# Branch-operand splits tied behind a weight and taken later; the low parts of all weights formed on VectorE

## The chip, the cores and the metric

The kernel runs on one core of one Trainium2 chip. The metric is the device time of one execution in microseconds (us). The engines are TensorE (PE, matrix products), VectorE (DVE), ScalarE (ACT), GpSimd (POOL) and SyncE (SP, whose queue starts most of the loads and stores). Each runs its own list of instructions in order and waits for the others through semaphores. What the scheduler decides is the order within each list.

## What is computed

One layer of a hybrid encoder over two sequences of 256 tokens, 1024 channels, in fp32, cut to what matters here:

```
h = rmsnorm(x);  proj = h @ w_in      -> qkv, ab, z_gdn, cq, ckv, z_mla, q_mem, z_mem, gate_logits
A: q,k,v = silu(conv5(qkv));  o_f, o_b = gated_delta_rule (chunks of 64, forward and backward), 8 heads
   o_gdn = rmsnorm(o_f + o_b) * silu(z_gdn)
B: latent attention, 8 heads, rotary keys, full softmax            o_mla = ... * silu(z_mla)
C: cross-attention into 256 memory tokens, 4 heads                 o_mem = ... * silu(z_mem)
merged = sig(g0)*(o_gdn @ w_br_gdn) + sig(g1)*(o_mla @ w_br_mla) + sig(g2)*(o_mem @ w_br_mem)
y = rmsnorm(x + merged @ w_out)
```

## The kernel before

All 512 tokens lie on the free axis and channels on the 128 partitions, so a product of one weight tile has 128 output channels by 512 tokens. Each fp32 operand is held as a rounded high part and a low part (operand minus high part). A product is three passes: high activations times high weight (`hh`, `wh`), low activations times high weight (`hl`, `wh`), high activations times low weight (`hh`, `wl`), 24 matmuls of 128x512 for 1024 input channels.

`weight` (L195) brings one weight tile in. SP loads it into the raw tile `wr_name` (two buffers), ACT rounds it to `wh_name` (two buffers, L206, remembered as `self.wround`), and one engine subtracts to form `wl_name` (two buffers, L213). That engine is POOL, in steps of 256 columns, for names that begin with q (`qkv`, `qm`, `qn`) and for `km3`; for the others it is DVE, in one instruction, which is remembered as `self.wsplit`. The next load into a raw buffer waits until both its rounding and its subtraction are done. `split` does the same for an activation: ACT writes the high part (L221), DVE the low part (L223, or L225 with a scale).

The program has three stages. `front` (to about 383 us) runs the memory attention, the latent attention (softmax tiles `p_m`, `ph_m`, `p_a`) and products between them; there the scheduler sets the order on all engines. `middle` (to about 745 us) is the gated delta rule. Its function `weave` merges chains of steps (lanes that solve heads, their loads, norms, the preparation of four heads at a time in `gdn_prep`) with a list of fill products. Each chain yields a planned time, the fill list fills the time between, and PE's order is written by hand from this. `back` has the last projections and the output. A convolution on a product tile is a copy `cz` (ACT L735), five shifted multiply-adds on DVE (`kq`, `vf`, L744 and L746) and copies on ACT.

A lane's solve goes back and forth between the engines: PE `u` (L1080), ACT `u` and `ub` (L1082, L1085), PE `xs` (L1090), DVE `w` (L1094), PE `us` (L1099), ACT `ub` (L1102), PE `o` and `x`, DVE `vs` (L1075). `gdn_prep` inverts triangular blocks on DVE with 31 pairs `tm`, `tt` (L870, L872), then transposes and copies into `t32` and `y32` (L893 to L901).

`xe` is the gated output of the memory branch and `xa` that of the latent attention. Both were written to HBM as `d_xm` and `d_xa`. `load_xe` and `load_xa` bring tiles back, `split_x` and `split_xa` halve and split them, and `branch_mem` (weights `be`) and `branch(1, ...)` (weights `bm`) multiply them with a branch weight. All are entries of the fill list; `can` says which may be taken at the planned time `now`: a `split_xa` of parts 0 to 4 when 6 planned us have passed since its load, a `split_x` at once when its turn comes. Instructions under `issue_after(i)` are placed behind instruction `i` in the order of their engine.

Of the kernel before, what the change touches and what calls it, by code (L numbers as in the profile page):

```python
# [7 lines left out]
F32 = mybir.dt.float32  # L8
F32R = mybir.dt.float32r
AF = mybir.ActivationFunctionType  # L10
ALU = mybir.AluOpType
# [4 lines left out]
D = 1024  # L16
KD = D // P
EPS = 1e-6
NEG = -1e30


# [19 lines left out]
def _consts():  # L41
# [8 lines left out]
    for tb in range(2):  # L50
# [8 lines left out]
        ("trf", m <= i32), ("trb", m >= i32), ("i32", m == i32),  # L59
        ("ngf", np.where(i32 > m, 0.0, NEG)), ("ngb", np.where(i32 < m, 0.0, NEG)),  # L60
        ("one", np.ones((P, 1))), ("hf", np.full((P, 4), -0.5)), ("ph", np.full((P, 16), 0.5)),
# [93 lines left out]
class Layer:  # L155
# [34 lines left out]
    def c(self, n):  # L190
        lo, hi = _OFF[n]
        return self.cst[:, lo:hi]


    def weight(self, src, n, name, pool=None):  # L195

        nc = self.nc
        raw = self.p0.tile([P, 1024], F32, tag="wr", bufs=2, name="wr_" + name)
        with self.tc.high_priority(offset=1000):
            d = nc.sync.dma_start(raw[:, :n], src)  # L200
        if name == "bg2":
            self.after = d.ins
        kw = {} if pool else {"tag": "wh", "bufs": 2}
        hi = (pool or self.p0).tile([P, 1024], F32R, name="wh_" + name, **kw)
        with self.tc.high_priority(offset=60):
            self.wround = nc.scalar.activation(hi[:, :n], raw[:, :n], AF.Copy).ins  # L206
            kw = {} if pool else {"tag": "wl", "bufs": 2}
            lo = (pool or self.p0).tile([P, 1024], F32R, name="wl_" + name, **kw)
            eng = nc.gpsimd if name[0] == "q" or name == "km3" else nc.vector
            step = 256 if eng is nc.gpsimd else n  # L210
            for q in range(0, n, step):
                t = slice(q, min(n, q + step))
                d = eng.tensor_tensor(lo[:, t], raw[:, t], hi[:, t].bitcast(F32), op=ALU.subtract)  # L213
            if eng is nc.vector:
                self.wsplit = d.ins
        return hi, lo
# [44 lines left out]
    def mean_cols(self, acc, n, name):  # L261
# [5 lines left out]
        r = self.p0.tile([P, 4], F32, tag="c4", bufs=4, name="ms_" + name)  # L267
        nc.vector.tensor_scalar(r, ss[:, 0:4], 1.0 / n, EPS, ALU.mult, ALU.add)
        return r
# [506 lines left out]
    def gdn_prep(self, g):  # L776
# [4 lines left out]
        nc, c = self.nc, self.c  # L781
# [33 lines left out]
        with self.tc.high_priority(offset=0 if g else 900):  # L815
            for h in range(4):
                for s in range(2):
                    for cc in range(2):
                        w = h * 4 + s * 2 + cc
                        for a in range(4):  # L820
                            t = slice(cc * P + 32 * a, cc * P + 32 * a + 32)
# [11 lines left out]
        nc.vector.tensor_reduce(k2, tmp, axis=AX.X, op=ALU.add)  # L833
        nc.vector.tensor_scalar(k2, k2, 4 * EPS, None, ALU.add)
        nc.vector.reciprocal(rc, k2)
# [14 lines left out]
        for d in range(2):  # L850
            t = self.tb(f"nd{g}{d}").rearrange("p (w i) -> p w i", i=32)
# [15 lines left out]
        for i in range(31):  # L867
            n, m = 31 - i, i + 1
# [5 lines left out]
        ts = self.pb.tile([P, 32, 32], F32, tag="blk", bufs=3, name=f"ts{g}")  # L874
# [14 lines left out]
        for a in range(4):  # L889
            r = slice(32 * a, 32 * a + 32)  # L890
            d = a % 2
            with self.tc.issue_after(self.wround):
                nc.scalar.activation(t32[r], (o2 if d else o1)[r, :, 16 * d:16 * d + 16].rearrange("p i u -> p u i"),  # L893
                                     AF.Copy)
            yield 0.0, 6.0 if g else 2.8
        with self.tc.issue_after(self.wround):
            nc.scalar.activation(y32[:, 0:16], o2[:, :, 0:16].rearrange("p i u -> p u i"), AF.Copy)
        yield 0.0, 6.0 if g else 2.8
        for q in range(2):
            with self.tc.issue_after(self.wround):  # L900
                nc.scalar.activation(y32[:, 16 + q:32:2], o1[:, :, 17 - q:32:2].rearrange("p i u -> p u i"), AF.Copy)  # L901
            yield 0.0, 6.0 if g else 2.8
        self.ready[g] = self.now + 4
        return t32, y32, cc

# [18 lines left out]
    def decay_mask(self, es):  # L924
        for d, e in enumerate(es):
# [3 lines left out]
            for r in (slice(o, o + 128), slice(256, 384)):  # L929
                self.nc.gpsimd.affine_select(out=e[:, :, r], in_=e[:, :, r], pattern=[[0, 2], [sg, 128]],  # L930
                                             compare_op=ALU.is_ge, fill=NEG, base=0, channel_multiplier=-sg)

# [173 lines left out]
    def gdn_out(self, hh):  # L1106
# [33 lines left out]
        rr = self.rr[:, 0:4]  # L1140
        nc.vector.tensor_scalar(rr, ssp[:, 0:4], 1.0 / 128, 128 * EPS * EPS, ALU.mult, ALU.add)  # L1141
        nc.gpsimd.tensor_tensor(rr, rr, c("hf")[:, 0:4], op=ALU.pow)  # L1142
# [92 lines left out]
    def output(self):  # L1235
# [26 lines left out]
        def add(ps, tb, half, n=512):  # L1262
            y = ys[tb][:, half * n:(half + 1) * n]
            nc.vector.tensor_tensor(y, y, ps, op=ALU.add)
            i = half if n == 512 else half - 1
            nc.scalar.activation(self.ct("jk")[:, :n], y, AF.Square, accum_out=ss[tb][:, i:i + 1])
            return y
# [7 lines left out]
        for tb in range(4):  # L1275
            y = add(pss[tb], tb, 0)
            nc.vector.tensor_scalar(ss[tb][:, 0:1], ss[tb][:, 0:1], 1.0 / D, EPS, ALU.mult, ALU.add)
            nc.gpsimd.tensor_tensor(y, y, fg[:, 0:512], op=ALU.mult)
# [225 lines left out]
    def can(self, f, *a):  # L1504

        if f == self.load_xa:
            return (3 in self.ub and self.pr[1], 5 in self.ub and 7 in self.hd, 6 in self.ub and 7 in self.hd,
                    7 in self.started, self.out > 6 and 7 in self.started, 7 in self.ub)[a[0]]
        if f == self.split_xa:
            return self.now > self.xa_at.get(a[0], 1e9)  # L1510
        if f == self.branch_mem and a[0] == 7:
            return 5 in self.xa_raw
        return f != self.branch or None not in self.xa
# [42 lines left out]
    def load_xe(self, f):  # L1556

        t = self.big(f, f"xe{f}")
        self.nc.sync.dma_start(t[:, 1].bitcast(F32), self.d_xm[:, f])
        self.xe.append((t[:, 0], t[:, 1]))  # L1560
        yield 0.0

    def split_x(self, xs):
        for hi, lo in xs:
            self.split(lo.bitcast(F32), hi, lo, 0.5)
        yield 0.0

    def load_xa(self, part):

        lo, tags = ((0, ("y32",)), (1, ("na",)), (2, ("na", "y0")), (4, ("y32",)), (5, ("ub",)), (6, ("na", "y1")))[part]  # L1570
        ts = [self.pg.tile([P, 2, 512], F32R, tag=t, bufs={"na": 3, "y0": 1, "y1": 1}.get(t, 2), name=f"xa{f}")
              for f, t in enumerate(tags, lo)]
        for f, t in enumerate(ts, lo):
            self.nc.sync.dma_start(t[:, 1].bitcast(F32), self.d_xa[:, f])
        self.xa_at[part] = self.now + 6.0 if part < 5 else self.now
        self.xa_raw[part] = ts, lo
        yield 0.0

    def split_xa(self, part):
        ts, lo = self.xa_raw[part]  # L1580
        for f, t in enumerate(ts, lo):
            self.xa[f] = t[:, 0], t[:, 1]
            self.split(t[:, 1].bitcast(F32), t[:, 0], t[:, 1], 0.5)
        yield 0.0


# [22 lines left out]
```

## Time and profile before

| | us |
|---|---|
| median of 3 runs | 887.36 (886.44 to 888.58) |
| profiled execution, its own time | 888.98 |
| span of its trace, first to last instruction | 887.0 |
| PE busy | 861.5 (97%) |
| DVE busy | 547.0 (62%) |
| ACT busy | 471.0 (53%) |
| POOL busy | 225.7 (25%) |
| mean granted TensorE clock | 0.986 |

Spans and rows are those of the profiled execution, 1.62 us above the median. The granted clock is the share of full speed that TensorE was given. The idle time in square brackets at the end of a row is that of the engine just before this instruction, followed by what ended it.

### The profile page before, as it was taken

The page shows a single profiled execution, that of the slowest core. Times are in us where ns is not written, and L with a number is a line of the kernel's source. Part 1 is how long each engine was busy: PE and PEld are TensorE (multiplying, and loading weights), DVE is VectorE, ACT ScalarE, POOL GpSimd, SP SyncE. Part 2 cuts the span into 40 slices and gives each one's busy share as a digit, 9 for nine tenths or more (in the row PEclk, how much of TensorE's full clock was granted, in tenths as well). Part 3 has the DMA queues.
Part 4 walks back from the last instruction along what each step waited for, and adds up shares of the span by engine and source line. Part 5 has one row for each costly group of instructions (what it writes and reads, how often), then busy time and mean ns, then how long its engine had stood idle before and what let it go on. Part 6 is the DMA issues. An engine that isn't in the chain of part 4 may idle for free.

```text
span 887.0 us, 13366 instructions
## 1 busy us (share of the span) xinstructions
PE 861.5 (97%) x4854; PEld 709.0 (80%) x4854; DVE 547.0 (62%) x976; ACT 471.0 (53%) x915; POOL 225.7 (25%) x251
## 2 busy tenths in 40 slices
PE   9999999989999999999999999999999989999997
PEld 7878888778888878878788878888788868888886
DVE  7775437856789866336789975593355543335643
ACT  7645445445464555584675787766364532213332
POOL 0250352321303221254224242611110000432221
PEclk9999999999999999999999999999999999999999
DMA  9322222442225324462333455544433445565422
GB/s 333 118 89 84 78 71 64 133 128 84 82 89 173 110 91 129 152 201 86 109 94 117 140 140 162 172 138 131 136 128 119 143 143 173 184 197 206 119 95 95
DMA packets 50865, 116.10 MB, mean 131 GB/s; under 512 B 7152, under 2 KB 12656, under 8 KB 50800
## 3 DMA queue, kind: packets, MB, share of 16 engines
q1 hardware_dynamic: 44896, 104.51, 36.9%
q10 hardware_dynamic: 5904, 10.75, 3.4%
q8 instruction: 38, 0.62, 0.3%
q14 instruction: 27, 0.22, 0.1%
HBM read 95.09 MB, written 16.99 MB: 126 GB/s over the span
## 4 chain that ended last, share of the span: by engine, by line
PE 71%; DVE 14%; DMA 5%; ACT 4%; issue 2%; POOL 2%; SPq 1%; ACTq 0%; DVEq 0%; POOLq 0%
PE gm_g L245 11%; PE gm_qkv L245 8%; PE gm_bm L245 5%; PE gm_bg L245 5%; PE y L1258 4%; PE gm_za L245 4%; PE gm_z L245 4%; PE vm L398 3%; PE gm_be L245 3%; PE gm_qm L245 3%; PE gm_km L245 3%; DVE tm L870 2%; DVE tt L872 2%; PE s_a L307 2%; PE gm_cq L245 2%
## 5 line engine op out<-in xcount | busy, mean ns | idle before, releaser
L213 POOL TENSOR_TENSOR wl_qkv<-wr_qkv,wh_qkv 128x256 fp32r<-128x256 f32 x96 | 79.0, 852 | 123.2 <-ACT wh_qkv L206 39.2
L744 DVE SCALAR_TENSOR_TENSOR kq<-cz,prm,kq 128x510 f32<-128x510 f32 (+1 forms) x64 | 51.2, 800 | 27.8 <-ACT kq L737 27.3
L245 PE MATMUL gm_g<-hh,wh_g 128*128 128x512 f32 x192 | 53.6, 415 | 2.7 <-ACT cz L735 2.7
L245 PE MATMUL gm_g<-hh,wl_g 128*128 128x512 f32 x192 | 54.6, 408 | 0.0
L245 PE MATMUL gm_qkv<-hh,wh_qkv 128*128 128x512 f32 x192 | 52.1, 407 | 1.5 <-ACT wh_qkv L206 0.8
L245 PE MATMUL gm_qkv<-hh,wl_qkv 128*128 128x512 f32 x192 | 51.0, 397 | 0.0
L245 PE MATMUL gm_g<-hl,wh_g 128*128 128x512 f32 x192 | 50.5, 398 | 0.0
L245 PE MATMUL gm_qkv<-hl,wh_qkv 128*128 128x512 f32 x192 | 49.8, 396 | 0.0
L213 DVE TENSOR_TENSOR wl_g<-wr_g,wh_g 128x1024 fp32r<-128x1024 f32 x24 | 30.0, 1248 | 28.3 <-ACT wh_g L206 11.7
L245 PEld LDWEIGHTS gm_g<-hh,wh_g 128*128 128x128 f32 x192 | 36.3, 195 | 10.7 <-ACT cz L735 3.1
L245 PEld LDWEIGHTS gm_qkv<-hh,wh_qkv 128*128 128x128 f32 x192 | 35.8, 194 | 9.7 <-ACT wh_qkv L206 1.2
L1228 POOL TENSOR_TENSOR mg<-mg,lg 128x512 f32<-128x512 f32 x16 | 28.8, 1801 | 56.4 <-DVE lg L1227 49.1
L245 PEld LDWEIGHTS gm_qkv<-hl,wh_qkv 128*128 128x128 f32 x192 | 35.8, 188 | 8.2
L245 PEld LDWEIGHTS gm_g<-hl,wh_g 128*128 128x128 f32 x192 | 35.8, 190 | 8.0
L245 PEld LDWEIGHTS gm_g<-hh,wl_g 128*128 128x128 f32 x192 | 35.9, 193 | 7.4
L245 PEld LDWEIGHTS gm_qkv<-hh,wl_qkv 128*128 128x128 f32 x192 | 35.3, 188 | 7.6
L1258 PE MATMUL y<-wh_wo,mh 128*128 128x512 f32 (+1 forms) x144 | 40.0, 370 | 0.0
L206 ACT ACTIVATE wh_qkv<-wr_qkv 128x1024 fp32r<-128x1024 f32 x24 | 25.3, 1055 | 23.6 <-PE gm_qkv L245 7.9
L1142 POOL TENSOR_TENSOR rr<-rr,cst 128x4 f32<-128x4 f32 x8 | 8.1, 1009 | 113.1 <-DVE rr L1141 113.1
L206 ACT ACTIVATE wh_g<-wr_g 128x1024 fp32r<-128x1024 f32 x24 | 25.3, 1054 | 20.3 <-PE gm_g L245 11.1
L963 POOL TENSOR_TENSOR kl<-kq,kh 128x512 fp32r<-128x512 f32 x16 | 20.6, 1291 | 47.6 <-ACT kh L961 42.8
L245 PE MATMUL gm_bm<-xa,wh_bm 128*128 128x512 f32 x128 | 32.4, 395 | 0.0
(434 smaller groups left out, 2260.7 us busy)
## 6 DMA issues: line engine op xcount, KB each, us to landing
wr_qkv<-in_w_dram SPq DMA_DIRECT2D x24, 512.0 KB
wr_g<-in_w_dram SPq DMA_DIRECT2D x24, 512.0 KB
e<-d_r SPq DMA_DIRECT2D x64, 96.0 KB
wr_z<-in_w_dram SPq DMA_DIRECT2D x12, 512.0 KB
wr_za<-in_w_dram SPq DMA_DIRECT2D x8, 512.0 KB
d_g<-gt_g ACTq DMA_DIRECT2D x16, 256.0 KB
wr_bm<-in_w_dram SPq DMA_DIRECT2D x8, 512.0 KB
lg<-d_g SPq DMA_DIRECT2D x16, 256.0 KB
```

The lines of the kernel that those rows point to most:

```text
L206: self.wround = nc.scalar.activation(hi[:, :n], raw[:, :n], AF.Copy).ins
L213: d = eng.tensor_tensor(lo[:, t], raw[:, t], hi[:, t].bitcast(F32), op=ALU.subtract)
L245: nc.tensor.matmul(ps[:m], a[:, k * m:(k + 1) * m], xs[k][j], start=n == 0, stop=n == 3 * nk - 1)
L307: nc.tensor.matmul(sp[:, qb * 256:(qb + 1) * 256], a, b, start=j == 0, stop=j == n - 1)
L398: nc.tensor.matmul(vps[tb], ms[k][a][:, t], b[:, :512], start=k == 0 and i == 0, stop=k == 7 and i == 2)
L744: nc.vector.scalar_tensor_tensor(ys, zs, self.cw[:, f, m:m + 1], ys, ALU.mult, ALU.add)
L870: nc.vector.tensor_tensor(t3, xx[:, m:, i:i + 1].to_broadcast([P, n, m]), tt[:, i:i + 1, 0:m].to_broadcast([P, n, m]), op=ALU.mult)
L872: nc.vector.tensor_tensor(tt[:, m:, 0:m], tt[:, m:, 0:m], t3, op=ALU.add)
L963: nc.gpsimd.tensor_tensor(lo, src, hi.bitcast(F32), op=ALU.subtract)
L1142: nc.gpsimd.tensor_tensor(rr, rr, c("hf")[:, 0:4], op=ALU.pow)
L1228: nc.gpsimd.tensor_tensor(self.merged[d], self.merged[d], gt, op=ALU.add)
L1258: nc.tensor.matmul(ps, xs[2 * j + q][a][:, t], b[:, q * 512 + c0:q * 512 + c1], start=j == 0 and n == 0, stop=j == 3 and n == 5)
```

## The change

Four edits. In `weight`, the subtraction of every weight is one DVE instruction, so each weight also sets `self.wsplit`. `split_x` and `split_xa` put their instructions behind the latest weight rounding on ACT. `split_xa` of parts 0 to 4 may be taken 14 planned us after its load instead of 6, and `split_x` 14 planned us after the last `load_xe` instead of at once. The copies at the end of the second `gdn_prep` are planned 4.5 us apart instead of 6.

```diff
+XAT = 14.0
...
-            eng = nc.gpsimd if name[0] == "q" or name == "km3" else nc.vector
-            step = 256 if eng is nc.gpsimd else n
-            for q in range(0, n, step):
-                t = slice(q, min(n, q + step))
-                d = eng.tensor_tensor(lo[:, t], raw[:, t], hi[:, t].bitcast(F32), op=ALU.subtract)
+            eng = nc.vector
+            d = eng.tensor_tensor(lo[:, :n], raw[:, :n], hi[:, :n].bitcast(F32), op=ALU.subtract)
             if eng is nc.vector:
                 self.wsplit = d.ins
...
-            yield 0.0, 6.0 if g else 2.8
+            yield 0.0, 4.5 if g else 2.8
...
+        if f == self.split_x:
+            return self.now > self.xe_at
...
         self.xe.append((t[:, 0], t[:, 1]))
+        self.xe_at = self.now + XAT
...
     def split_x(self, xs):
-        for hi, lo in xs:
-            self.split(lo.bitcast(F32), hi, lo, 0.5)
+        with self.tc.issue_after(self.wround):
+            for hi, lo in xs:
+                self.split(lo.bitcast(F32), hi, lo, 0.5)
...
-        self.xa_at[part] = self.now + 6.0 if part < 5 else self.now
+        self.xa_at[part] = self.now + XAT if part < 5 else self.now
...
-        for f, t in enumerate(ts, lo):
-            self.xa[f] = t[:, 0], t[:, 1]
-            self.split(t[:, 1].bitcast(F32), t[:, 0], t[:, 1], 0.5)
+        with self.tc.issue_after(self.wround):
+            for f, t in enumerate(ts, lo):
+                self.xa[f] = t[:, 0], t[:, 1]
+                self.split(t[:, 1].bitcast(F32), t[:, 0], t[:, 1], 0.5)
```

What this moves, at three places (numbers behind names are the program's own and differ between the two kernels). First, ACT where the gate of the last memory tile (`d_g`) has been stored and a lane's `u` and `ub` stand. Before:

```order
L1198 DMA d_g<-gt_g_6342 128x512
L221 ACTIVATE xe_6427<-xe_6427 128x512
L1082 ACTIVATE u_6380<-u_6377 128x256
L1085 ACTIVATE ub_6376<-u_6377 64x2x128 x2
L206 ACTIVATE wh_z_6492<-wr_z_6490 128x1024
L1164 ACTIVATE zt_z_6417<-gm_z_6351 128x512
```

And now:

```order
L1196 DMA d_g<-gt_g_6247 128x512
L1080 ACTIVATE u_6285<-u_6282 128x256
L1083 ACTIVATE ub_6281<-u_6282 64x2x128 x2
L207 ACTIVATE wh_z_6397<-wr_z_6395 128x1024
L219 ACTIVATE xe_6326<-xe_6326 128x512
L219 ACTIVATE xe_6328<-xe_6328 128x512
L219 ACTIVATE xe_6330<-xe_6330 128x512
L219 ACTIVATE xe_6332<-xe_6332 128x512
L1162 ACTIVATE zt_z_6322<-gm_z_6256 128x512
```

The lane's `u` and `ub` and the next weight's rounding stand ahead of the `xe` split, and all four `xe` tiles stand in one row; the first three were at three earlier places.

Second, DVE around the first of those earlier places, with the convolution of a value tile (`vf`) and the lane's `w`. Before:

```order
L213 TENSOR_TENSOR wl_z_5312<-wr_z_5308,wh_z_5310 128x1024
L744 SCALAR_TENSOR_TENSOR vf_5159<-cz_5160,prm,vf_5159 128x2x254
L225 SCALAR_TENSOR_TENSOR xe_6421<-xe_6421 128x512
L744 SCALAR_TENSOR_TENSOR vf_5159<-cz_5160,prm,vf_5159 128x2x254
L1094 TENSOR_TENSOR w_5283<-vs_3870,xs_5278 128x256
L746 SCALAR_TENSOR_TENSOR vf_5159<-cz_5160,vf_5159 128x512
```

And now, where `o` are the two transposes at the end of the second `gdn_prep`:

```order
L211 TENSOR_TENSOR wl_z_5231<-wr_z_5227,wh_z_5229 128x1024
L744 SCALAR_TENSOR_TENSOR vf_5077<-cz_5078,vf_5077 128x512
L876 STREAM_TRANSPOSE o_4916<-ts_4864 128x1024
L878 STREAM_TRANSPOSE o_4918<-tt 128x1024
L1092 TENSOR_TENSOR w_5201<-vs_3808,xs_5196 128x256
L1153 TENSOR_TENSOR og_4976<-og_4976,rob_5216 128x512
L211 TENSOR_TENSOR wl_qkv_5350<-wr_qkv_5346,wh_qkv_5348 128x1024
```

The `xe` split is gone from ahead of `w`; the two transposes, which stood ahead of this piece, are now directly ahead of `w`, and the low part of a `qkv` weight stands behind it.

Third, DVE in `front` where the first gate weight `wr_g` is loaded, during the convolution of a key tile (`kq`). Before, with the low parts of the `qkv` and `qn` weights in POOL's list:

```order
L744 SCALAR_TENSOR_TENSOR kq_1289<-cz_1703,prm,kq_1289 128x2x255 x2
L223 TENSOR_TENSOR vl_1731<-v_1723,vh_1730 128x512
L744 SCALAR_TENSOR_TENSOR kq_1289<-cz_1703,prm,kq_1289 128x2x254
L223 TENSOR_TENSOR kn_1747<-gm_kn_1740,kn_1747 128x512
L744 SCALAR_TENSOR_TENSOR kq_1289<-cz_1703,prm,kq_1289 128x2x254
L746 SCALAR_TENSOR_TENSOR kq_1289<-cz_1703,kq_1289 128x2x256
L213 TENSOR_TENSOR wl_g_1827<-wr_g_1823,wh_g_1825 128x1024
```

And now:

```order
L742 SCALAR_TENSOR_TENSOR kq_1271<-cz_1673,prm,kq_1271 128x2x255 x2
L211 TENSOR_TENSOR wl_qkv_1724<-wr_qkv_1720,wh_qkv_1722 128x1024
L221 TENSOR_TENSOR vl_1701<-v_1693,vh_1700 128x512
L742 SCALAR_TENSOR_TENSOR kq_1271<-cz_1673,prm,kq_1271 128x2x254
L221 TENSOR_TENSOR kn_1717<-gm_kn_1710,kn_1717 128x512
L211 TENSOR_TENSOR wl_qn_1765<-wr_qn_1761,wh_qn_1763 128x384
L742 SCALAR_TENSOR_TENSOR kq_1271<-cz_1673,prm,kq_1271 128x2x254
L211 TENSOR_TENSOR wl_g_1793<-wr_g_1789,wh_g_1791 128x1024
```

The two subtractions stand between the steps of the convolution, and the subtraction of the gate weight stands ahead of the convolution's last step.

Over the whole program POOL's list loses the subtractions of 37 weights (24 `qkv`, 4 `qm`, `km3` and 8 `qn`) and DVE's gains as many. PE's order differs in many places up to about 383 us and is the same from there to the end. The ACT order of the last `xa` parts, around the last lane's `u`, is the same as before.

## Rows read from the trace of the kernel before

**Rows 1.** The page's first part: span, then busy time, share of the span and instructions of each engine.

```profile
span 887.0 us, 13366 instructions
PE 861.5 (97%) x4854; PEld 709.0 (80%) x4854; DVE 547.0 (62%) x976; ACT 471.0 (53%) x915; POOL 225.7 (25%) x251
```

**Rows 2.** PE's timeline, some of the rows that show idle time before them: start and duration in us, engine, line, operation, tiles, count, and in brackets the idle time before with what ended it.

```profile
136.05 0.81 PE L333 MATMUL pt_m<-cst,p_m 128*128 128x128 f32 x4 [0.33 <-DVE p_m L329]
137.54 0.39 PE L342 MATMUL om<-ph_m,vmh 128*128 128x256 f32 x1 [0.69 <-ACT ph_m L221]
186.15 3.63 PE L245 MATMUL gm_g<-hh,wh_g 128*128 128x512 f32 x8 [2.66 <-ACT cz L735]
520.40 0.71 PE L1099 MATMUL us<-w,y 128*128 128x128 f32 x4 [1.61 <-DVE w L1094]
562.51 2.11 PE L245 MATMUL gm_z<-hh,wh_z 128*128 128x512 f32 x8 [0.46 <-DVE e L984]
629.18 0.68 PE L1090 MATMUL xs<-u,m 128*128 128x128 f32 x4 [1.98 <-ACT ub L1085]
725.32 0.68 PE L1080 MATMUL u<-vs,y 128*128 128x128 f32 x4 [1.03 <-DVE vs L1075]
731.35 1.19 PE L1099 MATMUL us<-w,y 128*128 128x128 f32 x4 [1.36 <-DVE rt L287]
```

**Rows 3.** Stretches of 5 and 20 us: length, busy time and count of PE, PEld, DVE, ACT and POOL, then the granted clock, the DMA share and GB/s.

```profile
135.00:140.00 5.00, 3.64 (x21) 2.88 (x20) 4.96 (x11) 2.70 (x8) 0.52 (x1) 0.86 0.38 120
140.00:145.00 5.00, 5.00 (x23) 4.31 (x23) 4.43 (x15) 2.03 (x6) 0.95 (x1) 0.80 0.01 3
185.00:190.00 5.00, 3.85 (x10) 3.03 (x11) 4.61 (x7) 2.00 (x4) 0.00 (x0) 0.66 0.44 145
...
630.00:635.00 5.00, 5.00 (x19) 4.14 (x18) 2.25 (x4) 1.45 (x4) 0.12 (x1) 0.66 0.36 124
...
280.00:300.00 20.00, 20.00 (x88) 16.15 (x87) 19.64 (x37) 8.72 (x15) 4.99 (x6) 1.00 0.47 140
```

**Rows 4.** ACT's timeline around 627 us and SP's load of the tile that it waits for.

```profile
624.03 0.33 SPq L1559 DMA_DIRECT2D xe<-d_xm  x1
...
627.61 0.63 ACT L221 ACTIVATE xe<-xe 128x512 fp32r<-128x512 f32 x1 [9.14 <-DMA xe<-d_xm]
628.40 0.75 ACT L1085 ACTIVATE ub<-u 64x256 f32<-64x256 f32 x2
```

**Rows 5.** DVE's timeline around 518 us, with one of the transposes that come before.

```profile
510.25 1.20 DVE L880 STREAM_TRANSPOSE o<-tt 128x1024 f32<-128x1024 f32 x1
...
518.66 0.69 DVE L225 SCALAR_TENSOR_TENSOR xe<-xe 128x512 fp32r<-128x512 f32 x1 [2.73 <-ACT xe L221]
519.93 0.41 DVE L1094 TENSOR_TENSOR w<-vs,xs 128x256 f32<-128x256 f32 x1
```

**Rows 6.** The end of the second `gdn_prep`: its last copy on ACT, and PE's first product of head 4, the first that reads its tiles.

```profile
521.79 0.67 ACT L901 ACTIVATE y<-o 128x256 f32<-128x256 f32 x1
...
569.38 0.45 PE L1024 MATMUL p<-t,na 32*32 32x32 f32 x32
```

**Rows 7.** ACT's timeline at 555 us and 728 us, where a tile of `xa` is split.

```profile
555.26 0.63 ACT L221 ACTIVATE xa<-xa 128x512 fp32r<-128x512 f32 x1 [0.85 <-DMA xa<-d_xa]
...
727.93 0.63 ACT L221 ACTIVATE xa<-xa 128x512 fp32r<-128x512 f32 x1 [3.12 <-DMA xa<-d_xa]
```

**Rows 8.** The stretch from 175 to 186 us, in order of time: POOL's subtraction, SP's load of the first gate weight, ACT's rounding of it, and the copy that frees PE's next output tile.

```profile
175.57 4.25 POOL L213 TENSOR_TENSOR wl_qkv<-wr_qkv,wh_qkv 128x256 fp32r<-128x256 f32 x4 [9.05 <-ACT wh_qkv L206]
...
179.84 0.33 SPq L200 DMA_DIRECT2D wr_g<-in_w_dram  x1
...
183.68 1.06 ACT L206 ACTIVATE wh_g<-wr_g 128x1024 fp32r<-128x1024 f32 x1 [3.74 <-DMA wr_g<-in_w_dram]
...
185.52 0.58 ACT L735 ACTIVATE cz<-gm_qkv 128x512 f32<-128x512 f32 x1
```

**Rows 9.** DVE and PE in the same stretch: two steps of the convolution, and the last product ahead of PE's wait.

```profile
174.58 1.53 DVE L744 SCALAR_TENSOR_TENSOR kq<-cz,prm,kq 128x510 f32<-128x510 f32 x2
...
182.63 0.86 PE L245 MATMUL gm_qn<-qlh,wl_qn 128*128 128x512 f32 x3
```

**Rows 10.** All instructions of line 213 by tile: engine, operation, tiles, count, then minimum, median and maximum duration in ns, first and last start in us, shapes.

```profile
L213 POOL TENSOR_TENSOR wl_qkv<-wr_qkv,wh_qkv x96: 720/742/1285, 112.9 to 570.5; 128x256 fp32r<-128x256 f32 x96
...
L213 DVE TENSOR_TENSOR wl_za<-wr_za,wh_za x8: 1207/1225/1228, 194.4 to 361.4; 128x1024 fp32r<-128x1024 f32 x8
...
L213 DVE TENSOR_TENSOR wl_bg<-wr_bg,wh_bg x8: 1218/1781/2345, 786.0 to 825.4; 128x1024 fp32r<-128x1024 f32 x8
...
L213 DVE TENSOR_TENSOR wl_ra<-wr_ra,wh_ra x2: 551/555/559, 134.3 to 253.7; 128x384 fp32r<-128x384 f32 x2
```

**Rows 11.** DVE's and POOL's timeline between 484 and 492 us: steps of the second `gdn_prep` on DVE, beside a subtraction on POOL and after it.

```profile
484.69 3.37 POOL L213 TENSOR_TENSOR wl_qkv<-wr_qkv,wh_qkv 128x256 fp32r<-128x256 f32 x4 [2.20 <-PE gm_z L245]
...
485.73 0.85 DVE L872 TENSOR_TENSOR tt<-tt,tm 128x255 f32<-128x255 f32 x1
486.62 0.84 DVE L870 TENSOR_TENSOR tm<-xx,tt 128x252 f32<-128x252 f32 x1
487.49 0.85 DVE L872 TENSOR_TENSOR tt<-tt,tm 128x252 f32<-128x252 f32 x1
...
491.85 0.41 DVE L872 TENSOR_TENSOR tt<-tt,tm 128x240 f32<-128x240 f32 x1
```

More of the change, by code (lines that the diff above doesn't have):

```diff
@@ L894, in gdn_prep @@
                                      AF.Copy)
-            yield 0.0, 6.0 if g else 2.8
+            yield 0.0, 4.5 if g else 2.8
         with self.tc.issue_after(self.wround):
             nc.scalar.activation(y32[:, 0:16], o2[:, :, 0:16].rearrange("p i u -> p u i"), AF.Copy)
-        yield 0.0, 6.0 if g else 2.8
+        yield 0.0, 4.5 if g else 2.8
         for q in range(2):
@@ L901, in gdn_prep @@
                 nc.scalar.activation(y32[:, 16 + q:32:2], o1[:, :, 17 - q:32:2].rearrange("p i u -> p u i"), AF.Copy)
-            yield 0.0, 6.0 if g else 2.8
+            yield 0.0, 4.5 if g else 2.8
         self.ready[g] = self.now + 4
```

## The prediction

> **What bounds the kernel now.** I read the busy shares first: PE is busy 97% of the span and no other engine more than 62% [rows 1]. So time is lost only where PE idles, and where it runs at the lower of its two clock levels. I therefore went through PE's timeline for every row with idle time before it [rows 2], and through the span in stretches of 5 us for granted clocks below 1 [rows 3]. The reader is to see two things there. First, PE's waits are few, and most end on ACT or DVE, not on a load. Second, a wait of 2 us or more is followed by a lowered clock. After the 2.66 us wait at 186.15, eight matmuls take 3.63 us, and the stretch 185 to 190 has a granted clock of 0.66, so 0.34 x 5 = 1.70 us are lost on top of the wait. The stretch 630 to 635 behind the 1.98 us wait at 629.18 shows the same 0.66 [rows 2, 3]. Then for each wait I asked what the engine that ended it had done before.
>
> **The splits, after 383 us.** PE's order there is unchanged, so a gain can only be a wait that vanishes.
>
> At 629.18 PE waits 1.98 us for `xs`, whose operand `ub` comes from ACT at 628.40. ACT was idle for 9.14 us ahead of the `xe` split at 627.61, waiting for a tile that SP began to load at 624.03, and `u` and `ub` stood behind that split [rows 2, 4]. In the new order they stand ahead of it, so ACT can do them while that load is still under way. The price removed is 1.98 + 1.70 = 3.7 us. What is late next: the four `xe` splits now come together, 4 x 0.63 = 2.5 us on ACT from the landing at 627.6, and behind them `zt_z`, which before ran right behind the next weight's rounding and had no PE wait on it. I take the whole 3.7; the lower bound is 2.0, if the clock falls for another reason.
>
> At 520.40 PE waits 1.61 us for `us`, whose `w` DVE makes at 519.93, behind an `xe` split for which DVE sat idle 2.73 us [rows 2, 5]. That split is gone from there. But the two transposes that end the second `gdn_prep` (1.20 us each, the second at 510.25) now stand ahead of this `w`, and they need an ACT copy first. As an estimate: if that copy is done by 515.5, some 5 us after the transpose of before started, `w` ends at 515.5 + 2 x 1.20 + 0.41 = 518.3, against 520.40 - 1.61 = 518.79 at which PE asks for it. The margin is 0.5 us, so I take 1.3 of the 1.61, with 0 and 1.61 as bounds.
>
> At 562.51 PE waits 0.46 us for DVE, which had an `xa` split in front, itself behind an ACT wait of 0.85 us at 555.26 [rows 2, 7]. This split moves to a much later place: 0.4, between 0 and 0.46.
>
> The waits from 725.32 to 731.35 come from the last `xa` parts (ACT idle 3.12 us ahead of the one at 727.93, with the last lane's `u` behind it) [rows 2, 7]. That order is the same after the change, so the gain there is 0, although these are the longest waits left.
>
> The copies at 4.5 us instead of 6 cost and bring nothing. The preparation ends around 522 and is first read at 569.38 [rows 6]; these 47 us cover even the several us by which its steps move back.
>
> **The subtractions.** POOL loses 37 weights. Of these, 29 become a DVE instruction of 1024 columns at 1.225 us (`wl_za`) and 8 one of 384 columns at 0.555 us (`wl_ra`) [rows 10]: 29 x 1.225 + 8 x 0.555 = 35.5 + 4.4 = 40 us, and DVE would go from 547 to 587 us, two thirds of the span.
>
> What one weight gains is latency. Between 175 and 186 us the chain is this: POOL subtracts a `qkv` weight from 175.57 for 4.25 us. This frees the raw buffer, SP starts the load of `wr_g` at 179.84, ACT waits 3.74 us for it until 183.68, and the copy `cz` that frees PE's output tile stands behind that rounding, at 185.52 [rows 8]. PE had issued its last product at 182.63 (0.86 us) and idles to 186.15 [rows 2, 9]. In the new order DVE subtracts behind the two steps that end at 174.58 + 1.53 = 176.11 [rows 9], so to about 177.3. The load starts 2.5 us earlier, `wh_g` is rounded from about 181.2, and `cz`, now directly behind it and one short copy, starts at about 182.9. PE's wait of 2.66 shrinks to about 0, and the clock stays up: 2.66 + 1.70 = 4.4 us. If `cz` were only 2 us earlier, 2.7 would be left of this; if DVE is late, 0. I take 4.4.
>
> What DVE pays depends on the place. In the middle its spare time is small, but there the subtraction on POOL already costs DVE time: beside the one from 484.69 to 488.06, three steps took 0.84 to 0.85 us each, and a like one afterwards 0.41 [rows 11]. Four such steps give back 4 x 0.44 = 1.8 us for the 1.22 that the new instruction takes. So per weight DVE's net lies between a gain of 0.5 us and a loss of 1.22, and I take 0 for the middle. In `front`, 135 to 140 us has DVE busy 4.96 of 5 us, and 280 to 300 us 19.64 of 20 [rows 3]; one more weight of 1.22 us ahead of a softmax step at each of two such places is 2.5 us of new PE wait. The scheduler also rearranges PE there, which I can't price; the bounds are the waits seen around 136 us (0.33 + 0.69, and a clock loss of (0.14 + 0.20) x 5 = 1.7 [rows 2, 3]), once gained and once again lost: 2.7 us either way. I take the 2.5 as a loss.
>
> The Trainium skill bears on this (page "SBUF — State Buffer", section "Who interferes with whom"): a VectorE instruction with two SBUF inputs and a GpSimd instruction that reads SBUF exclude each other, and whichever comes second waits out the whole instruction. It speaks against any two-input subtraction on DVE beside POOL's work. The rows agree in direction: `wl_bg` takes 1.78 us in the median where `wl_za` takes 1.225 [rows 10]. By the rule alone, were each of the 37 blocked like the median `wl_bg`, DVE would be busy 37 x 0.56 = 21 us longer, some 608 us; the sum below goes by the 1.225, and the difference would be beside PE's products except in the places of rival (c).
>
> The sum: 3.7 + 1.3 + 0.4 + 4.4 = 9.8 us gained, 2.5 given back, 7.3 us net. The profiled execution took 888.98 us and would take 881.7. The median of the runs, 887.36, is 1.62 lower and becomes **880.1 us**.
>
> **Rivals.**
> (a) Only the splits work. DVE reaches the `qkv` subtraction at 176 us too late, because its list is full, and `wr_g` is loaded no earlier. Gains 3.7 + 1.3 + 0.4 = 5.4, front given back 2.5: 884.5 us. For it: the convolution steps stand one behind the other there. Against it: the new order puts the subtraction behind only two of them.
> (b) `front` eats the gain. The 5.4 us of the splits are met by a rearranged front that loses twice the 2.7 of the place at 136 us: 5.4 - 5.4 = 0, 887.4 us. That the splits don't reach their waits, because ACT arrives late at the same `u` for another reason, would end here too.
> (c) VectorE becomes the bound, and the kernel is slower. DVE is full around 135 to 140 and 280 to 300 us; three to five further weights in each stretch come ahead of the softmax results, 4 x 1.22 = 4.9 us late at each. If PE has no other product there, both waits show in full with a clock loss of 1.7 us each: 13.2 us lost against 5.4 gained, 895 us. It decides from about 7.2 us of new PE idle time in front. Against it: PE waited only 0.69 us at most at 136 us, and not at all from 280 to 300 us, with DVE full [rows 2, 3].
> (d) More is gained: no give-back, and the 2.7 us at 136 us vanish as well, since DVE is rid of POOL beside it: 887.36 - 9.8 - 2.7 = 874.9 us.
>
> **How the numbers follow.** Chances: forecast 0.45, (a) 0.22, (b) 0.12, (c) 0.12, (d) 0.09. The predicted time is that of the forecast. Leaving out (c) and most of (d), the range reaches from 875.5 to about the end of (b), 888. About 0.2%, 1.8 us, is what a measurement of this kernel can tell from no change. Forecast, (a) and (d) are faster by more: 0.76. (b) is the same: 0.12. (c) is slower: 0.12.
>
> **What would show it.** Right: no PE wait at `xs` around 622 to 629 us after the `xe` wait, which itself stays on ACT with nothing of the lane behind it; clock 1.00 in that stretch and around 185 us; the load of `wr_g` some 2.5 us nearer to the rounding of the weight ahead of it; POOL busy at most 225.7 - 96 x 0.742 = 154 us (the `qkv` weights alone [rows 10]), DVE between 547 and 587. The waits of the tail stay as they are. Wrong: a new PE wait above 1 us ended by a softmax tile in front, a wait on `w` near 518 us behind the two transposes, or a lane's `vs` behind a subtraction. The term that I trust least is the front's 2.5, since PE's order there is new.

## The result and the profile after

The changed kernel takes 878.45 us (median of 4 runs, 877.71 to 882.74) against 887.14 us for the kernel before (4 runs): a ratio of 0.9908, 95% interval 0.9878 to 0.9937. The forecast was 880.1 us in a range of 875.5 to 888. The profiled execution of after took 877.71 us with a span of 875.9. The spans of the two profiles differ by 11.1 us and the medians by 8.7, so 2.4 us of what these two traces show is chance of single executions.

The first part of the page of after, to be held against [rows 1]:

```profile
span 875.9 us, 13248 instructions
PE 855.2 (98%) x4854; PEld 705.2 (81%) x4854; DVE 564.1 (64%) x1013; ACT 472.5 (54%) x915; POOL 120.1 (14%) x119
```

POOL lost 106 us. DVE got 37 instructions more and is busy only 17 us longer, where the price list said 40.

PE's timeline of after, rows with idle time before them, to be held against [rows 2]:

```profile
140.77 0.80 PE L331 MATMUL pt_m<-cst,p_m 128*128 128x128 f32 x4 [1.50 <-DVE p_m L327]
182.66 2.12 PE L243 MATMUL gm_g<-hh,wh_g 128*128 128x512 f32 x8 [0.55 <-ACT cz L733]
515.56 2.45 PE L1121 MATMUL o<-e,ub 128*128 128x128 f32 x14 [3.01 <-ACT ub L1100]
713.32 0.68 PE L1078 MATMUL u<-vs,y 128*128 128x128 f32 x4 [1.04 <-DVE vs L1073]
717.28 1.22 PE L1088 MATMUL xs<-u,m 128*128 128x128 f32 x4 [0.75 <-ACT u L1080]
719.73 1.19 PE L1097 MATMUL us<-w,y 128*128 128x128 f32 x4 [1.23 <-DVE rt L285]
```

The waits at 520, 562 and 629 us are gone, the one at 186 us fell from 2.66 to 0.55, and the tail kept its waits. New is the longest wait of all: 3.01 us at 515.56 for a lane's `ub`.

To see where the 11.1 us lie, take two marks that stand at the same place of PE's order in both kernels: the first product `p` of the lanes, and the last `x` of the last lane. From PE's timeline, in us (the first `p` lies some 40 us behind the end of `front`, and in these 40 us neither profile has a PE wait of 0.1 us or more):

| kernel | first `p` (front) | last `x` | from `p` to `x` (middle) | span |
|---|---|---|---|---|
| before | 422.84 | 723.23 | 300.39 | 887.0 |
| after | 413.89 | 711.22 | 297.33 | 875.9 |
| weights_only | 413.88 | 716.91 | 303.03 | 880.9 |
| splits_only | 419.97 | 716.23 | 296.26 | 880.0 |
| after_again | 415.11 | 716.22 | 301.11 | 879.4 |

The front gave 8.95 us and the middle 3.06; the end took 0.9 back, and the granted clock there was 0.51 and 0.50 from 715 to 725 us. The middle's gain is that of one execution: `after_again`, the same kernel profiled once more, has 7.73 us in front and a middle that is 0.72 us longer than that of before. The last three rows are experiments, told below.

ACT's timeline of after around the `xe` splits, to be held against [rows 4]:

```profile
612.52 0.38 ACT L1080 ACTIVATE u<-u 128x256 f32<-128x256 f32 x1 [2.03 <-PE u L1078]
612.80 0.76 ACT L1083 ACTIVATE ub<-u 64x256 f32<-64x256 f32 x2
613.58 1.06 ACT L207 ACTIVATE wh_z<-wr_z 128x1024 fp32r<-128x1024 f32 x1
614.54 1.66 ACT L219 ACTIVATE xe<-xe 128x512 fp32r<-128x512 f32 x3
619.08 0.63 ACT L219 ACTIVATE xe<-xe 128x512 fp32r<-128x512 f32 x1 [2.88 <-DMA xe<-d_xm]
```

ACT still waits for the tile, 2.88 us now, but the lane's `u` and `ub` run 6 us ahead of it, and PE's `xs` found them ready.

DVE, SP and ACT of after around the first gate weight, to be held against [rows 8]:

```profile
174.53 1.22 DVE L211 TENSOR_TENSOR wl_qkv<-wr_qkv,wh_qkv 128x1024 fp32r<-128x1024 f32 x1
...
175.78 0.51 SPq L201 DMA_DIRECT2D wr_g<-in_w_dram  x1
...
180.55 1.06 ACT L207 ACTIVATE wh_g<-wr_g 128x1024 fp32r<-128x1024 f32 x1 [4.75 <-DMA wr_g<-in_w_dram]
181.51 0.62 ACT L743 ACTIVATE cz<-kq 128x512 f32<-128x512 f32 x1
182.04 0.57 ACT L733 ACTIVATE cz<-gm_qkv 128x512 f32<-128x512 f32 x1
```

The subtraction takes 1.22 us where POOL took 4.25. The load behind it starts 4.1 us earlier and takes 4.8 us to arrive where it took 3.8, so the rounding gains 3.1 us.

After ahead of the new wait, first the PE product that the late `ub` needs and DVE's last transpose of the preparation, then ACT:

```profile
504.57 0.61 PE L1097 MATMUL us<-w,y 128*128 128x128 f32 x4
...
507.19 1.20 DVE L878 STREAM_TRANSPOSE o<-tt 128x1024 f32<-128x1024 f32 x1
...
507.30 2.34 ACT L891 ACTIVATE t<-o 32x512 f32<-32x512 f32 x2 [0.79 <-DVE o L876]
509.65 1.21 ACT L899 ACTIVATE y<-o 128x256 f32<-128x256 f32 x2
510.76 1.04 ACT L207 ACTIVATE wh_qkv<-wr_qkv 128x1024 fp32r<-128x1024 f32 x1
511.83 2.19 ACT L891 ACTIVATE t<-o 32x512 f32<-32x512 f32 x2
514.04 1.07 ACT L895 ACTIVATE y<-o 128x512 f32<-128x512 f32 x1
515.13 0.78 ACT L1100 ACTIVATE ub<-us 64x256 f32<-64x256 f32 x2
```

Two lanes are under way here, and each `us` is copied into the `ub` of its lane in turn: the `us` of 504.57 by the copy at 515.13, the next one (at 509.65) by a copy at 516.93. So the late `ub` had its product from 505.2 on. ACT copies it only at 515.13, since the preparation's copies, over 1 us each for a `t`, stand ahead of it.

### The profile page after: what moved, and what is told of

Same layout as the page of the kernel before. It is cut to its first block, busy times and chain, and to the rows that moved or that the text cites. A ratio compares the mean times of both kernels' runs of the same rounds, so it can differ in the third digit from the quotient of the medians.

```text
span 875.9 us, 13248 instructions
## 1 busy us (share of the span) xinstructions
PE 855.2 (98%) x4854; PEld 705.2 (81%) x4854; DVE 564.1 (64%) x1013; ACT 472.5 (54%) x915; POOL 120.1 (14%) x119
## 4 chain that ended last, share of the span: by engine, by line
PE 92%; ACT 3%; DVE 2%; DMA 2%; issue 1%; POOL 0%; POOLq 0%; DVEq 0%; ACTq 0%; SPq 0%
PE gm_g L243 16%; PE gm_qkv L243 14%; PE gm_z L243 7%; PE gm_bm L243 5%; PE gm_bg L243 5%; PE gm_za L243 5%; PE y L1256 4%; PE vm L396 3%; PE o L1121 3%; PE gm_be L243 3%; PE gm_qm L243 3%; PE gm_km L243 3%; PE kk L971 2%; PE s_a L305 2%; PE gm_cq L243 2%; PE gm_qn L243 2%
## 5 line engine op out<-in xcount | busy, mean ns | idle before, releaser
L742 DVE SCALAR_TENSOR_TENSOR kq<-cz,prm,kq 128x510 f32<-128x510 f32 (+1 forms) x64 | 47.8, 747 | 13.3 <-ACT kq L735 12.6
L243 PE MATMUL gm_g<-hh,wl_g 128*128 128x512 f32 x192 | 51.8, 400 | 0.0
L211 DVE TENSOR_TENSOR wl_qkv<-wr_qkv,wh_qkv 128x1024 fp32r<-128x1024 f32 x24 | 30.0, 1249 | 26.7 <-ACT wh_qkv L207 12.2
L243 PE MATMUL gm_bg<-xg,wh_bg 128*128 128x512 f32 x128 | 32.4, 394 | 0.0
```

The costliest lines, as they stand in the source:

```text
L211: d = eng.tensor_tensor(lo[:, :n], raw[:, :n], hi[:, :n].bitcast(F32), op=ALU.subtract)
L243: nc.tensor.matmul(ps[:m], a[:, k * m:(k + 1) * m], xs[k][j], start=n == 0, stop=n == 3 * nk - 1)
L742: nc.vector.scalar_tensor_tensor(ys, zs, self.cw[:, f, m:m + 1], ys, ALU.mult, ALU.add)
```

## The experiments

All times are medians beside runs of the kernel before on the same chip. The ratios are estimated from all runs and can differ from the quotient of the two medians by some 0.0005.

| kernel | us | before beside it | ratio, 95% interval |
|---|---|---|---|
| weights_only | 882.29 | 889.10 | 0.9925, 0.9904 to 0.9945 |
| splits_only | 885.10 | 889.10 | 0.9955, 0.9938 to 0.9973 |
| spacing6 | 879.07 | 889.10 | 0.9891, 0.9873 to 0.9909 |
| untied | 882.66 | 889.10 | 0.9933, 0.9916 to 0.9949 |
| front_dve | 875.58 | 887.97 | 0.9863, 0.9843 to 0.9882 |
| one_weight | 885.23 | 887.97 | 0.9966, 0.9953 to 0.9979 |
| tieub | 875.00 | 887.97 | 0.9853, 0.9833 to 0.9874 |
| tail | 876.36 | 887.97 | 0.9874, 0.9855 to 0.9892 |
| after_again | 879.41 | 888.06 | 0.9903, 0.9884 to 0.9921 |
| tieub_tail | 873.30 | 888.06 | 0.9831, 0.9813 to 0.9850 |
| front_tail | 873.62 | 888.06 | 0.9841, 0.9822 to 0.9861 |

**Which half does what.** `weights_only` is the kernel before with the edit in `weight` alone; `splits_only` is the kernel before with `XAT`, the new `can` and the two `issue_after`, and nothing else.

> The kernel before with the subtractions of all weights on VectorE and nothing else; TensorE's order is that of the changed kernel. Theory (the front gains through the weights, the middle through the splits): the front ends about 8 us earlier, the wait for ub near 515 us (3.0 us in the changed kernel) appears, and the waits behind the xe splits stay; about 882 us, some 5 below the kernel before. Rival (the gain is the splits' and the front's shorter time in the one profile is a chance of the clock): 886 to 888 us.

> The kernel before with the splits tied and delayed and nothing else; TensorE's order is that of the kernel before everywhere. Theory: the waits at 520, 562 and 629 us go (1.6 + 0.46 + 2.0, and 1.7 of clock), the front stays; about 882 us, 5.4 below the kernel before. Rival (splits carry the whole gain): about 878.5 us.

The weights alone give 6.8 us and the splits alone 4.0 (5.4 were expected), and the sum of 10.8 is about what both give on that chip (`spacing6`: 10.0). The marks show that they act in different stages: with the weights the front ends at 413.88 as in after, with the splits alone at 419.97. PE's timeline of `weights_only`:

```profile
515.66 4.64 PE L1120 MATMUL o<-e,ub 128*128 128x128 f32 x14 [3.12 <-ACT ub L1099]
622.79 0.68 PE L1087 MATMUL xs<-u,m 128*128 128x128 f32 x4 [0.96 <-ACT ub L1082]
631.30 0.71 PE L1096 MATMUL us<-w,y 128*128 128x128 f32 x4 [1.35 <-DVE w L1091]
```

The new wait near 515 us is there without any moved split. Its price is not only 3.1 us: the 14 products behind it take 4.64 us where after shows 2.45, because they ran at the lower clock (granted clock 0.50 from 515 to 520 us). The waits at the `xe` split are there too. The middle of `weights_only` is 2.6 us longer than that of the kernel before. PE's timeline of `splits_only`:

```profile
141.60 0.80 PE L334 MATMUL pt_m<-cst,p_m 128*128 128x128 f32 x4 [1.21 <-DVE p_m L330]
...
186.23 2.12 PE L246 MATMUL gm_g<-hh,wh_g 128*128 128x512 f32 x8 [2.18 <-ACT cz L736]
...
519.29 2.45 PE L1124 MATMUL o<-e,ub 128*128 128x128 f32 x14 [0.65 <-ACT ub L1103]
...
630.63 0.71 PE L1100 MATMUL us<-w,y 128*128 128x128 f32 x4 [0.65 <-DVE w L1095]
```

Here the front's waits are all still there; the middle is 4.1 us shorter than before. The waits at 520, 562 and 629 us are gone, and two smaller ones of 0.65 us came in their place. The rival, that the front's gain was chance, falls.

**Delay or tie.** `untied` keeps the 14 us and takes the tie away:

```diff
     def split_x(self, xs):
-        with self.tc.issue_after(self.wround):
-            for hi, lo in xs:
-                self.split(lo.bitcast(F32), hi, lo, 0.5)
+        for hi, lo in xs:
+            self.split(lo.bitcast(F32), hi, lo, 0.5)
```

(and the same in `split_xa`).

> The changed kernel with the 14 planned us kept but without the tie behind a weight's rounding: on ScalarE the xe splits stand again at four scattered places, the last one ahead of a lane's u and ub. Theory (the tie moves the splits, the delay does not): the wait for ub at xs near 618 us is back with 2 us and the lower clock, and a split stands near the transposes at 508 us; 882 to 883 us. Rival (the delay is what matters): 878.5 us.

882.66 us, the time of `weights_only`. The traces of the two show the same order on ACT and DVE, but for one copy `y` near 511 us: the scheduler puts the four `xe` splits back at their scattered places, although they are planned 14 us later, and the waits return:

```profile
621.54 0.68 PE L1088 MATMUL xs<-u,m 128*128 128x128 f32 x4 [0.62 <-ACT ub L1083]
630.52 0.71 PE L1097 MATMUL us<-w,y 128*128 128x128 f32 x4 [1.81 <-DVE w L1092]
```

So the tie moves the splits. Whether the tie would do without the 14 us, no run shows. In the numbers the expectation was off: the wait at `xs` is 0.62, not 2, and the larger one is 9 us later at `us`.

**What makes the new wait.** `spacing6` has the copies 6 us apart again.

> The changed kernel with the last copies of the second preparation planned 6 us apart again; on ScalarE one copy moves behind a weight's rounding, nothing else moves. Theory (the new wait for ub near 515 us comes from the preparation being tied to more weights and so later): within 0.2% of the changed kernel, about 878.5 us, and the wait of about 3 us stays. Rival (the closer spacing made that wait): 3 us less, about 875.5 us.

879.07 us, and the wait is 3.17 us: the closer spacing neither made it nor mended it. `front_dve` subtracts the `qkv` weights on GpSimd again from the middle on, in steps of 256 columns as before:

```diff
-            eng = nc.vector
+            eng = nc.gpsimd if name[0] == "q" and hasattr(self, "ym") else nc.vector
...
```

> The changed kernel, but from the start of the middle on the qkv weights are subtracted on GpSimd again, as before; the front keeps VectorE. Theory (in the middle the subtractions on VectorE push the second preparation back, and its ScalarE copies then stand ahead of a lane's ub): the 3 us wait near 515 us is gone, the front still ends at its first product of the lanes near 414 us, the middle is as long as with the splits alone; about 876 us, 3 below the changed kernel. Rival (VectorE, rid of GpSimd beside it, is what makes the middle fast): no faster than the changed kernel, 878.5 or more.

875.58 us, with the front's first `p` at 414.68 and the wait down to 0.48:

```profile
514.01 2.45 PE L1124 MATMUL o<-e,ub 128*128 128x128 f32 x14 [0.48 <-ACT ub L1103]
```

`tieub` leaves the subtractions on DVE and moves only the copies on ACT, behind a lane's `ub` and 8 planned us later:

```diff
-        yield 0.0, 4.0
+        yield 0.0, 12.0 if g else 4.0
...
-            with self.tc.issue_after(self.wround):
+            with self.tc.issue_after(self.usub if g else self.wround):
```

(the tie three times, for all these copies), where `usub` is the last copy of an `us` into `ub`.

> The changed kernel with the last copies of the second preparation placed behind a lane's last us copy into ub on ScalarE and started 8 planned us later; VectorE and TensorE keep their order. Theory (the copies of 1.1 us each ahead of ub are what TensorE waits for near 515 us): the wait falls from 3 us to about 1, about 876.5 us. Rival (VectorE's late transposes hold the chain): the wait stays, 878.5 us.

875.00 us. ACT now makes the copy between two of the preparation's copies, and PE goes on without a wait (the same 16 products in one row):

```profile
511.64 1.20 ACT L891 ACTIVATE t<-o 32x512 f32<-32x512 f32 x1
512.87 0.78 ACT L1100 ACTIVATE ub<-us 64x256 f32<-64x256 f32 x2
513.67 1.09 ACT L891 ACTIVATE t<-o 32x512 f32<-32x512 f32 x1
```
```profile
512.82 2.93 PE L1121 MATMUL o<-e,ub 128*128 128x256 f32 x16
```

Together these two name the cause: the middle's subtractions on DVE move the end of the second preparation, and the order of ACT that comes with it has the copies ahead of `ub`. Held against the same place of PE's order, the last transpose of after comes 5.9 us later than in [rows 5] (507.19 + 8.97 - 510.25, where 8.97 us is the lead of after at the last lane product before it). DVE's lateness alone isn't what PE waits for: `tieub` has the same DVE order up to this product. Whether it is the time of the subtractions or the order that the scheduler makes around them which moves the preparation, no run separates.

**The gate weight at 186 us.** `one_weight` is the kernel before, with the one subtraction of [rows 8] on DVE.

```diff
-            eng = nc.gpsimd if name[0] == "q" or name == "km3" else nc.vector
+            eng = nc.gpsimd if (name[0] == "q" and name != "qkv16") or name == "km3" else nc.vector
```

> The kernel before with one weight alone subtracted on VectorE: the qkv weight that GpSimd had from 175.57 for 4.25 us, in whose raw buffer the first gate weight is loaded next. Theory (that subtraction held the load, the load held the copy behind it): TensorE's wait at 186 us falls from 2.2 to 2.7 us to about 0.5, all else the same; 1.7 to 4 us less than the kernel before. Rival (the front's gain comes from the new order of TensorE or from elsewhere): within 0.2% of the kernel before.

885.23 us, 2.7 less. In its trace ACT waits 1.24 us for the weight instead of 3.74, and PE's first product with it has no wait:

```profile
182.82 1.06 ACT L206 ACTIVATE wh_g<-wr_g 128x1024 fp32r<-128x1024 f32 x1 [1.24 <-DMA wr_g<-in_w_dram]
```
```profile
184.42 2.13 PE L245 MATMUL gm_g<-hh,wh_g 128*128 128x512 f32 x8
```

The chain from POOL's subtraction over the raw buffer and the load to PE is shown, at the price of the wait. The expectation had all else the same, but PE's order differs from that of before at some 20 places from 182 to 220 us. The gain lies ahead of nearly all of them: from PE's product `gm_qkv` at 175.54 to the gate weight's first product before took 10.61 us, and here, from 176.45, 7.97.

**The tail, and both repairs.** `tail` puts the splits of the last two `xa` parts behind the last lane's `ub` on ACT and behind its `w` on DVE, and lets them be taken only when this `w` has its place:

```diff
-            return self.now > self.xa_at.get(a[0], 1e9)
+            return self.now > self.xa_at.get(a[0], 1e9) and (a[0] < 4 or self.solved > 7)
...
+            with self.tc.issue_after(self.wround if part < 4 else self.uub):
+                nc.scalar.activation(t[:, 0], src, AF.Copy, scale=0.5)
+            with self.tc.issue_after(self.wround if part < 4 else self.wlast):
+                nc.vector.scalar_tensor_tensor(t[:, 1], src, 0.5, t[:, 0].bitcast(F32), ALU.mult, ALU.subtract)
```

> The changed kernel with the splits of the last two xa parts behind the last lane's ub on ScalarE and behind its w on VectorE. Theory (these splits wait for loads with the lane's u and w behind them, and that is the wait from 713 to 720 us): TensorE's waits for u and for w there fall by some 2 us, and less of it runs at the lower clock; 874.5 to 876.5 us. Rival (the tail is short of other work for TensorE, so the wait only moves behind): 878.5 us.

876.36 us. The wait of `xs` for `u` is gone, and the one at `us` fell from 1.23 to 0.66; those for `vs` and `sq` ahead of them (1.04 and 0.83) stay:

```profile
718.35 0.69 PE L1088 MATMUL xs<-u,m 128*128 128x128 f32 x4
719.70 1.19 PE L1098 MATMUL us<-w,y 128*128 128x128 f32 x4 [0.66 <-DVE w L1092]
```

> The changed kernel once more, beside the two candidates on one chip, for a second profile of it. Theory: the front ends near 414 us again and the wait for ub near 515 us is again about 3 us; 878 to 880 us. Rival (either was a chance of the one profile): the front ends above 418 us or the wait is under 1.5 us.

> The changed kernel with both repairs: the preparation's copies behind ub, and the last two xa parts behind the last lane's ub and w. Theory (the two waits are at different places and independent): their gains add, 3.5 + 2 us below the changed kernel, about 873 us. Rival (the lane with ub takes its time elsewhere): no better than the better of the two alone, 875 us.

> The kernel with GpSimd's subtractions in the middle and VectorE's in the front, and the last two xa parts behind the last lane's ub and w. Theory: 875.6 less 2 us, about 873.5 us. Rival: 875.5 us.

After once more: 879.41 us, first `p` at 415.11, wait 3.12, so neither was chance. The two repairs together take 873.30 us, 6.1 below after on the same chip; apart they had ratios of 0.9853 and 0.9874 against 0.9903 for after, 4.4 and 2.6 us, so the gains about add (7.0 against 6.1). `front_tail` takes 873.62, which the intervals don't tell from it. Both are faster than before and after.

## Why the forecast was right, step by step

The time came out 1.7 us below the forecast, but that it came so near is partly luck: three terms were wrong (the copies, the gate weight, the front's give-back), and their errors offset each other.

*The last `xe` split, 3.7 us*: right. The lead of after over before grows from 8.25 us at the lane product `x` near 607 us (607.11 against 598.86) to 12.00 at the next (644.75 against 632.75), so 3.75 us vanish there, wait and clock. In `after_again` and `splits_only` it is 2.9 us.

*The first `xe` split, 1.3 us, and the copies that "cost and bring nothing"*: the wait at 520 went, all 1.61 us of it, but the copies are the step that failed. The prediction looked only at who reads them (569 us) and not at what stands behind them on ACT. The new wait of 3.01 us takes more than the old one gave: the lead falls from 8.97 us at the `x` of 491.72 to 7.57 at that of 527.50. Instead of a gain of 1.3 that is a loss of 1.4, and in `after_again`, where the clock fell as well, this stretch takes 3.0 us more. `spacing6`, `front_dve` and `tieub` show that not the new spacing but the place of the copies, which comes with the subtractions, did it.

*The `xa` split, 0.4 us*: the wait at 562 is gone and the marks give 0.7 (7.57 to 8.25), but that the split did it is not shown. `weights_only`, where the split has its old place, gains the same 0.7 from the `x` of 527.50 to the next (47.24 against 47.92 us), `splits_only` 0.3.

*The gate weight, 4.4 us*: the mechanism is right and the size was too large. The load started 4.1 us earlier, not 2.5, but was longer under way. `one_weight` gives 2.7 us; the 1.7 for the clock isn't always lost there, as the trace of `splits_only` shows, where PE waits 2.18 us at the same place and the next eight products take 2.12 us.

*The front's give-back, 2.5 us*: wrong in sign. PE's idle time in front fell elsewhere too. The stretches of `splits_only` and after, which had full clock in front (columns as in [rows 3]):

```profile
180.00:246.00 66.00, 62.92 (x440) 52.20 (x439) 43.76 (x77) 36.18 (x72) 14.39 (x18) 1.00 0.30 99
246.00:320.00 74.00, 73.48 (x365) 60.59 (x363) 64.86 (x131) 40.14 (x77) 16.06 (x19) 1.00 0.39 120
320.00:383.00 63.00, 60.68 (x324) 50.91 (x323) 32.62 (x54) 37.33 (x75) 13.54 (x19) 1.00 0.44 140
```
```profile
180.00:246.00 66.00, 64.72 (x452) 53.58 (x451) 51.74 (x101) 39.02 (x79) 2.90 (x1) 1.00 0.28 94
246.00:320.00 74.00, 74.00 (x362) 61.20 (x361) 59.88 (x122) 40.34 (x73) 0.95 (x1) 1.00 0.40 125
320.00:383.00 63.00, 61.94 (x332) 52.34 (x331) 32.84 (x54) 41.64 (x80) 10.63 (x14) 1.00 0.47 139
```

In these three PE is busy 1.8, 0.5 and 1.3 us longer in after. From 246 to 320 us DVE, which was to be overloaded there, is busy 5 us less. The lane's mark moves by 6.1 us against `splits_only`; `one_weight` accounts for 1.6 of that (its first `p` is at 418.34). Which of the other weights bring the remaining 4.5, and how much of it comes from the new order of PE, no run separates. The 8.95 us against the profile of before hold 2.9 us on top, by which before and `splits_only` differ with the same front; before lost clock there [rows 3] and `splits_only` did not.

*The tail, 0*: about right. PE's four waits there sum to 4.2 us before and 3.9 after.

*Rivals.* (a) and (b) fall with `weights_only` and `splits_only`. (c), VectorE as the bound, falls with the time, with a front that got shorter and with DVE's 564 us. (d)'s reason, DVE rid of POOL beside it, is borne out by DVE's busy time, but the softmax waits of 136 to 142 us remain, the largest of 1.50. A new wait above 1 us behind a softmax tile was to be a sign that the prediction is wrong; this one is not new, since `splits_only`, with the front of before, has 1.21 us at the same product.

## What to carry to other kernels

Where a load waits for a subtraction that frees its buffer, the subtraction belongs on the engine that ends it first: its latency holds the next load, and the load holds whatever stands behind the rounding. Where no load waits, the same move can cost: in the middle it made the 3 us wait, and `front_dve`, which leaves those weights on GpSimd, was faster than the changed kernel. When moved work leaves all consumers with slack, also ask what is queued behind it on its own engine; the costliest wait of the new kernel was of that kind, and a tie with a later start removed it. To keep an operand's split from stalling a chain, fix its place in the engine's order, since a later planned time alone moved nothing.

## What was not expected of the hardware

DVE paid 17 us for 37 subtractions that take 40 us by their own rows. The subtractions took what they were priced at (median 1.225 us of 24); the rest got faster with POOL's subtractions gone. Groups of before and of after, all instances of one line and tile (count, then busy us and mean ns):

```profile
L744 DVE SCALAR_TENSOR_TENSOR kq<-cz,prm,kq 128x510 f32<-128x510 f32 (+1 forms) x64 | 51.2, 800 | 27.8 <-ACT kq L737 27.3
L870 DVE TENSOR_TENSOR tm<-xx,tt 128x31 f32<-128x31 f32 (+15 forms) x62 | 26.8, 432 | 1.0
```
```profile
L742 DVE SCALAR_TENSOR_TENSOR kq<-cz,prm,kq 128x510 f32<-128x510 f32 (+1 forms) x64 | 47.8, 747 | 13.3 <-ACT kq L735 12.6
L868 DVE TENSOR_TENSOR tm<-xx,tt 128x31 f32<-128x31 f32 (+15 forms) x62 | 23.6, 380 | 0.9
```

These two groups alone give back 6.6 us. It comes with the weights: the same two are busy 47.8 and 23.7 us in `weights_only`, 51.1 and 26.8 in `splits_only`. The prediction had this for the middle [rows 11] and not for the front. It is the direction of the rule cited there from the Trainium skill ("SBUF — State Buffer", "Who interferes with whom"), and it worked for the change, since it removed POOL's reader and not DVE's.

The 1.78 us of `wl_bg` in [rows 10] is a median between two kinds. Of its eight instructions before, four take 1.22 us and four 2.34 or 2.35. The long ones all start up to 0.03 us behind a two-input product on POOL (the one at 797.40 behind POOL's at 797.38, 1.29 us); the short ones all start ahead of it, and then POOL's takes 2.1 to 2.2 us instead of 1.29. After has five long ones, with the same pattern.

The prediction had the lower clock follow a wait of 2 us or more. It does not every time. Six profiles have the wait for `ub` near 515 us, of 3.0 to 3.2 us (after, `after_again`, `weights_only`, `spacing6`, `untied` and `tail`). In five of them the granted clock fell behind it; it stayed at 1.00 only in the profile of after. In that of `after_again` it was this (columns as in [rows 3]):

```profile
515.00:520.00 5.00, 3.12 (x10) 2.76 (x11) 2.22 (x5) 4.90 (x10) 0.32 (x1) 0.60 0.38 124
520.00:525.00 5.00, 5.00 (x25) 4.26 (x24) 3.94 (x9) 1.68 (x3) 0.95 (x1) 0.71 0.80 232
```

That is 0.40 x 5 + 0.29 x 5 = 3.4 us at most between two executions of one kernel. By the marks this stretch took 3.0 us more, most of why the middle took 301.11 us there and 297.33 in the first profile.
